# Second layer of a hybrid backbone: four gate projections of the first merge emitted inside the attention

## The chip, the cores and the metric

The kernel runs on one core of a Trainium2 chip. The metric is the device time of one execution in microseconds; lower is better. Engines are named as in the profile: PE is TensorE's matmul, PEld its weight load, DVE is VectorE, ACT is ScalarE, POOL is GpSimd, SP is the engine that issues the large loads.

## The reference

Two layers over 256 latent tokens and 256 context tokens, with a model width of 1024. Each layer has a mixing sub-layer with three branches on one normalised and modulated input h, and a convolutional feed-forward network. In the second (last) layer only the latent tokens go on, so most products have 256 columns there. The part that the change touches:

```python
cq, ckv, kr, uf, ur, ug, gl = split_in(h @ w_in)       # gl: 3 x 1024 gate logits
att = blocked_attention(q, k, v)                       # 8 heads, from cq, ckv, kr
g_att, g_f, g_rnn = split(sigmoid(gl), 3)
y = (g_att * (att @ w_o_attn)
     + g_f * (fourier_mix(uf) @ w_o_fourier)
     + g_rnn * (((h_f + h_b) * gelu(ug)) @ w_o_rnn)) @ w_out
```

fourier_mix is the real part of a two-dimensional DFT over positions and group channels; h_f and h_b come from gated linear recurrences over the tokens in both directions. All is float32; the kernel gets the precision on PE by splitting each operand into a rounded high part and a low part and adding three products.

## The kernel before

**Products.** gemm (L138) issues three matmuls per 128 rows of the contraction: high x high, high x low and low x high. A weight tile goes through three steps: load (L174) brings it from memory into one of three raw buffers by a load on SP's queue, and those loads are kept in program order (L165); unit (L193) takes one of three weight buffers (wp, wh and wl in the profile) and wsplit casts it on ACT (wh, L152) and subtracts on DVE (wl, L159); project (L605) multiplies eight such row blocks with h, 24 matmuls, into a bank of PSUM. columns (L199) loads 256 columns of a weight matrix at once, 1 MB, and gives two units of 128 columns, the second only when it is asked for.

**Order.** The program is written as generators, and what stands earlier in the program has the higher priority. A planner orders each engine's instructions at build time from its own estimates of time and from when buffers come free; on the chip each engine then keeps its fixed order. So an instruction that is emitted earlier is a candidate earlier; it isn't bound to the place where it stands.

**Second layer, attention (L861).** Eight heads, in four pairs p, are pipelined: step k of the loop emits the scores of head k (sc, then the softmax: nmx, pr, rs), the transposes of head k-1 (pt, split into pth and ptl) and the weighted values of head k-2 (pv, split into ath and atl). The one PSUM bank for pv is taken in turns. In steps 1, 3 and 5 the next pair's keys (kn) and queries (proj with nh, nl) are emitted with raised priority, with loads for their weights; step 3 also emits the second half of the values (v). At the end of step k, emit(fill, FILLS[l].get(k, 0)) (L974) advances a filler generator by so many steps. The filler is features (L762): the projection uf for the Fourier branch, in two halves of 256 columns; a half is three steps, one for the load and its two weight units, and one for each of two blocks of 128 tokens with 24 matmuls. For the second layer the table FILLS (L44) puts the first half into step 2 and the second half into step 8:

```python
FILLS = ({12: 1}, {2: 3, 8: 3})
```

**Second layer, branches (L1155).** fourier (L784) loads the DFT matrices (dft_l, dft_c), splits them (dlh, dll, dch) and forms fa and ff. Then recurrent (L979) runs beside the first two merges: each of its steps emits a gated recurrence (products gt, then tanh, exp, square root and scans on ACT, DVE and POOL) and the next convolved input (L996: two products with 512 and 256 columns, whose loads are issued at L1002); after it two steps of the merges follow. A step of merge (L1078) has two gate projections with tanh (sg, L1086), the product of the branch with two of its output tiles, and their product with the gate. The first merge is the Fourier branch's; its gates go straight into the eight M tiles. The attention's merge follows, and last the recurrence's. run(first_two, recurrent(rnn), 2) sets these two steps of merge per recurrence, so the first merge's first two steps (mp 0 and 1) go with the first recurrence.

**Memory.** phase (L94) opens tagged tiles in SBUF; the branches reuse the space of the attention's tiles. banks (L105) does the same for PSUM: three banks mm, two sc, one pt and one pv in the attention; three mg and four rc in the branches.

Of the kernel before, what the change touches and what calls it, by code (L numbers as in the profile page):

```python
# [12 lines left out]
F32 = mybir.dt.float32  # L13
F32R = mybir.dt.float32r
AF = mybir.ActivationFunctionType
# [4 lines left out]
D = 1024  # L20
# [18 lines left out]
C_UF, C_UR, C_UG, C_GL = 672, 1184, 1696, 2208  # L39
# [1 line left out]

HELD = (5, 8)

FILLS = ({12: 1}, {2: 3, 8: 3})  # L44


def constants():
# [23 lines left out]
def backbone(ctx: ExitStack, tc: tile.TileContext, a: dict, out: bass.AP):  # L71
    nc = tc.nc
# [7 lines left out]
    def nm(s):  # L80
        count[0] += 1
        return f"{s}_{count[0]}"
# [3 lines left out]
    def slot(s, tag="n", dtype=F32R, w=512):  # L86
        pool, bufs, tag = where[tag]
        return pool.tile([P, w], dtype, tag=tag, name=nm(s), bufs=bufs)

    def pair(s, tag, w=512):  # L90
        return slot(s + "h", tag, w=w), slot(s + "l", tag, w=w)

    @contextmanager
    def phase(name, **tags):  # L94

        with tc.tile_pool(name=nm(name), bufs=1, reuse_waits="tile") as pool:
            was = {t: where.get(t) for t in tags}
            where.update({t: (pool, n, t) for t, n in tags.items()})
            yield
            where.update(was)  # L100
# [14 lines left out]
    def bank(s, tag=None):  # L115
        pool, t, n = bank_of[tag or s]
        return pool.tile([P, 512], F32, tag=t, name=nm(s), bufs=n)
# [50 lines left out]
    def chain(*gens):  # L168
        for g in gens:
            yield from g  # L170
# [3 lines left out]
    def load(src, kt, c):  # L174
        if ticks:
            ticks[0]()
        return chunk(src.rearrange("(k p) c -> p k c", p=P), kt, c)
# [15 lines left out]
    def unit(v, tag=None):  # L193
        h, lo = wunit(v.shape[1], v.shape[2], tag)
        wsplit(h, lo, v)
        wmode["n"] += 1
        return h, lo

    def columns(w, c0, c1):  # L199

        kt = w.shape[0] // P
        for c in range(c0, c1, 256):
            n = min(256, c1 - c)
            v = load(w[:, c : c + n], kt, n)
            for j in range(0, n, P):
                yield unit(v[:, :, j : j + P])

    def run(main, side=None, every=1):

        while True:  # L210
            left = side is not None and next(side, True) is None
            for _ in range(every):
                if next(main, True) is not None and not left:
                    return
# [390 lines left out]
    def project(u, xs, r, parts=None, tag="mm"):  # L605

        hv, lv = u
        o = bank("proj", tag)[:, 0 : r.stop - r.start]
        for q in parts or [r]:
            oq = o[:, q.start - r.start : q.stop - r.start]  # L610
            gemm(oq, [(hv[:, k, :], lv[:, k, :], xs[k][0][:, q], xs[k][1][:, q]) for k in range(len(xs))])
        return o
# [4 lines left out]
    def mixer(l, col, ada_cols, last, h, tiles_of, steps, squares, first, then, open_banks):  # L617
        t0 = CTX if last else 0
        W = T - t0
        NS = W // CTX  # L620
        X, Y = slice(t0, T), slice(0, W)
        w_in = a["w_in"][l]
# [139 lines left out]
        def features(U, tag, where):  # L762

            for half in range(2):
                v = load(w_in[:, C_UF + half * 256 : C_UF + (half + 1) * 256], 8, 256)
                us = [unit(v[:, 0:4, :]), unit(v[:, 4:8, :])]
                yield
                f = slice(half * 256, (half + 1) * 256)
                for i in range(W // P):
                    r = slice(t0 + i * P, t0 + (i + 1) * P)  # L770
                    o = bank("uf", where)[:, 0:256]
                    gemm(
                        o,
                        [
                            (h[k][0][:, r], h[k][1][:, r], us[k // 4][0][:, k % 4, :], us[k // 4][1][:, k % 4, :])
                            for k in range(8)
                        ],
                    )
                    if half == 0:
                        U.append(pair("U", tag))  # L780
                    split(U[i][0][:, f], U[i][1][:, f], o)
                    yield
# [67 lines left out]
        def query_weights(p):  # L850
# [7 lines left out]
                wsplit(u[0][:, :, d0 : d0 + w], u[1][:, :, d0 : d0 + w], v[:, :, c0 : c0 + w])  # L858
            return u

        def attention(att, cq, ckvn, keys, pre, fill):  # L861
            vals, heads, cqn = {}, {}, []

# [96 lines left out]
            for k in range(len(items) + 2):  # L960
# [11 lines left out]
                if k == per + 1:  # L972
                    values(1, *kv)
                emit(fill, FILLS[l].get(k, 0))  # L974
                if k >= 2:
# [97 lines left out]
                    tile_0 = tile_1  # L1073
                    yield

        M, merged = [None] * 8, []

        def merge(b, br, wo, gofs):  # L1078

            for mp in range(4):  # L1080
                gu = columns(w_in, gofs + mp * 256, gofs + (mp + 1) * 256)
                sg = []
                for _ in range(2):
                    o = project(next(gu), h, X, None, "mg")
                    g = slot("sg", "M" if b == 0 else "sg", F32, W)
                    nc.scalar.activation(g, o, AF.Tanh, scale=0.5)  # L1086
                    sg.append(g)
                wu = unit(load(a[wo][l][:, mp * 256 : (mp + 1) * 256], 4, 256))
                for z in range(2):
                    m = 2 * mp + z  # L1090
                    c = slice(z * P, (z + 1) * P)
                    o = project((wu[0][:, :, c], wu[1][:, :, c]), br, Y, None, "mg")
                    g = sg[z]
                    nc.vector.scalar_tensor_tensor(g, g, 1.0, o, op0=ALU.add, op1=ALU.mult)
                    if b == 0:
                        M[m] = g
                    elif b == 1:
                        nc.gpsimd.tensor_tensor(M[m], M[m], g, op=ALU.add)
                    else:
                        nc.vector.tensor_tensor(M[m], M[m], g, op=ALU.add)  # L1100
                        hi, lo = slot("mh", "br", w=W), slot("ml", "att", w=W)
                        split(hi, lo, M[m])
                        merged.append((hi, lo))
                yield
# [21 lines left out]
        att, rnn, lats = [], [], []  # L1126
# [6 lines left out]
            next(lat)  # L1133
            yield
        U = []
        with phase("mix", att=8, **(dict(U=4) if last else {})):
            if last:
                tags = dict(rope=2, key=8, val=4, cqn=6, ckvn=4, q=6, pr=4, pt=8)
            else:
                tags = dict(rope=2, key=8, val=6, cqn=6, ckvn=4, q=4, pr=4, pt=4)  # L1140
            with phase("mla", **tags):
                load_rope()
                next(lat)
                lat_banks.close()
                with banks(dict(rb="mm", ss="mm"), mm=3, sc=2, pt=1, pv=1):
                    fill = features(U, *(("U", "mm") if last else ("M", "mg")))
                    run(attention(att, *lats, fill))
                    if last:
                        emit(fill)
            tags = dict(M=8, br=16 if last else 12)  # L1150
            if last:
                inner = dict(rg=1, sg=2, gw=4, u=6, ri=7, av=3, hd=4, ug=1)
            else:
                inner = dict(rg=1, sg=2, gw=2, u=3, ri=4, av=2, hd=2, ug=1)
            with phase("branch", **tags), banks(dict(rb="mg", ss="mg", out="rc"), mg=3, rc=4):  # L1155
                with phase("inner", **inner):
                    if not last:
                        emit(fill)
                    four = fourier(U)
                    if not last:  # L1160
                        wmode["hi"] = [nc.vector]
                    if last:
                        spread(steps, 0.5)
                    first_two = chain(merge(0, four, "w_o_fourier", C_GL + D), merge(1, att, "w_o_attn", C_GL))
                    run(first_two, recurrent(rnn), 2)
                    wmode["hi"] = [nc.scalar]
                    run(merge(2, rnn, "w_o_rnn", C_GL + 2 * D))
                    emit(steps)
                    ticks.clear()
                    units = ahead(out_units(), 2)  # L1170
                with phase("out", wo=2 * (8 - HELD[l])):
                    project_out(units)
# [233 lines left out]
    h = [pair("h", "h") for _ in range(8)]  # L1406
# [3 lines left out]
    def first_tiles(part):  # L1410
# [8 lines left out]
    mix = mixer(  # L1419
        0, columns_of[0], adas[0], False, h, first_tiles, chain(par0, ada(0, 1), ada(0, 2)), sq_ffn,  # L1420
        lambda: ups.append(ahead(columns(a["w_up"][0], 0, DFF))), lambda r: then[0](r), lambda: lat_banks,
    )
# [34 lines left out]
    for b in range(1, 3):  # L1457
# [9 lines left out]
    mix = mixer(  # L1467
        1, columns_of[1], adas[1], True, h_mix, lambda half: None, iter(()), sq_ffn,
        lambda: ups1.append(ahead(columns(a["w_up"][1], 0, DFF))), to_ffn, latent_banks,
    )  # L1470
# [29 lines left out]
```

## Time and profile before

| what | value |
|---|---|
| runs without profile | 1379.17, 1380.52, 1381.95 us; median 1380.52 us |
| the profiled execution, its own time | 1378.18 us |
| span of its profile | 1376.4 us |
| busy share of the span: PE, PEld, DVE, ACT, POOL | 97%, 83%, 68%, 50%, 15% |

The span runs from the first to the last instruction of the profiled execution; all positions below are microseconds from its start. In it the second layer's attention lies at about 918 to 991 us, the Fourier branch's DFT at 991 to 998, the recurrence and the first two merges at 998 to 1109, the third merge and the output projection behind that until 1172. A matmul's end is modelled, so its duration in a row (0.28 us for 256 columns) is longer than the distance from one start to the next.

### The profile page before, as it was taken

Reading aid. Unit: us, or ns where it says so; the run is one execution under the profiler, and the core shown is the slowest. Engines: PE = TensorE matmul, PEld = TensorE weight load, DVE = VectorE, ACT = ScalarE, POOL = GpSimd, SP = SyncE. Lnnn points to the kernel's source line nnn. Section 1 sums busy time; section 2 is a strip of 40 time slices with the busy share of each in tenths; the row PEclk is TensorE's granted clock in tenths of the full one; section 3 lists DMA queues with packets and bytes.
Section 4 is the critical chain, followed back from the end, with each engine's and each line's share of the span. In section 5 each row is a group of like instructions: output and inputs, shape, how many; then the busy total and the mean of one; then the engine's idle time right before and its main releaser. Section 6 shows DMA issues by size and latency. Waiting matters only on the chain.

```text
span 1376.4 us, 20199 instructions
## 1 busy us (share of the span) xinstructions
PE 1338.5 (97%) x7949; PEld 1148.8 (83%) x7949; DVE 931.7 (68%) x1528; ACT 688.9 (50%) x1165; POOL 200.8 (15%) x194
## 2 busy tenths in 40 slices
PE   7999999999999999999999999999999999999997
PEld 6777698888888798888888787978899999999996
DVE  3587646567644555579976786659777776766666
ACT  5476625335522434444421235457587855655555
POOL 2020002002120040101100011201012322111111
PEclk9999999999999999999999999999999999999999
DMA  9433652323233412245567764221255556455551
GB/s 330 141 104 143 247 152 65 112 80 92 81 104 107 153 36 93 92 135 171 152 183 252 269 214 131 72 73 52 71 156 146 165 156 210 150 189 179 189 189 72
DMA packets 177472, 196.42 MB, mean 143 GB/s; under 512 B 9285, under 2 KB 155699, under 8 KB 175329
## 3 DMA queue, kind: packets, MB, share of 16 engines
q1 hardware_dynamic: 176048, 193.23, 43.9%
q0 software_dynamic: 1328, 1.90, 0.4%
q8 instruction: 62, 1.02, 0.3%
q14 instruction: 34, 0.27, 0.1%
HBM read 194.06 MB, written 1.05 MB: 142 GB/s over the span
## 4 chain that ended last, share of the span: by engine, by line
PE 79%; DVE 9%; DMA 6%; ACT 4%; issue 2%; POOL 0%; SPq 0%; ACTq 0%; DVEq 0%; POOLq 0%
PE proj L130 49%; PE out L130 7%; PE acc L130 4%; DMA raw<-in_w_ada_dram 4%; PE lat L130 4%; DVE wl L159 3%; PE uf L130 2%; PE pa L130 2%; PE pv L130 2%; PE gt L130 1%; PE sc L130 1%; DVE acc L453 1%; PE pt L924 1%; DVE hf L564 1%; ACT wh L152 1%
## 5 line engine op out<-in xcount | busy, mean ns | idle before, releaser
L159 DVE TENSOR_TENSOR wl<-raw,wh 128x1024 fp32r<-128x1024 f32 (+9 forms) x337 | 336.9, 1014 | 154.6 <-ACT wh L152 152.0
L130 PE MATMUL proj<-hh,wl 128*128 128x512 f32 (+1 forms) x1232 | 415.1, 337 | 2.1 <-DVE wl L159 2.1
L130 PE MATMUL proj<-hh,wh 128*128 128x512 f32 (+1 forms) x1232 | 415.4, 338 | 0.0
L130 PE MATMUL proj<-hl,wh 128*128 128x512 f32 (+1 forms) x1232 | 414.9, 337 | 0.0
L152 ACT CAST wh<-raw 128x1024 fp32r<-128x1024 f32 (+7 forms) x305 | 248.1, 837 | 258.4 <-PE proj L130 149.9
L130 PEld LDWEIGHTS proj<-hh,wl 128*128 128x128 f32 x1232 | 233.6, 190 | 27.8 <-DVE wl L159 3.2
L130 PEld LDWEIGHTS proj<-hh,wh 128*128 128x128 f32 x1232 | 233.5, 190 | 25.5 <-issue 0.8
L130 PEld LDWEIGHTS proj<-hl,wh 128*128 128x128 f32 x1232 | 233.6, 190 | 25.4 <-DVE hl L566 0.2
L1370 POOL TENSOR_TENSOR gate<-gate,up 128x512 f32<-128x512 f32 (+1 forms) x44 | 57.7, 1312 | 460.2 <-ACT gate L1369 446.0
L453 DVE SCALAR_TENSOR_TENSOR acc<-raw,cvec,acc 128x512 f32<-128x512 f32 x112 | 88.6, 808 | 9.8 <-DMA raw<-in_w_ada_dram 8.6
L159 DVE TENSOR_TENSOR gTl<-gate,gTh 128x512 fp32r<-128x512 f32 (+1 forms) x44 | 24.4, 555 | 51.1 <-ACT gTh L152 51.0
L1369 ACT ACTIVATE gate<-gate 128x512 f32<-128x512 f32 (+1 forms) x44 | 23.1, 524 | 71.5 <-DVE gate L1225 71.5
L531 POOL TENSOR_TENSOR sq<-sq,sq 128x256 f32<-128x256 f32 (+1 forms) x22 | 26.2, 1189 | 176.5 <-ACT sq L529 176.4
L152 ACT CAST gTh<-gate 128x512 fp32r<-128x512 f32 (+1 forms) x44 | 22.6, 514 | 49.6 <-POOL gate L1370 49.6
L130 PE MATMUL out<-mh,wl 128*128 128x256 f32 (+1 forms) x152 | 47.4, 312 | 0.0
L130 PE MATMUL out<-ml,wh 128*128 128x256 f32 (+1 forms) x152 | 47.4, 312 | 0.0
L130 PE MATMUL out<-mh,wh 128*128 128x256 f32 (+1 forms) x152 | 47.4, 313 | 0.0
L154 DVE CAST wh<-raw 128x1024 fp32r<-128x1024 f32 x32 | 22.3, 698 | 33.3 <-PE proj L130 32.7
L130 PE MATMUL down<-gTh,wh 128*128 128x512 f32 x112 | 44.0, 393 | 0.0
L130 PE MATMUL down<-gTh,wl 128*128 128x512 f32 x112 | 43.7, 390 | 0.0
L130 PE MATMUL down<-gTl,wh 128*128 128x512 f32 x112 | 43.6, 389 | 0.0
L130 PE MATMUL lat<-hh,wh 128*128 128x512 f32 (+3 forms) x108 | 39.0, 361 | 0.6 <-ACT hh L565 0.6
(312 smaller groups left out, 2720.9 us busy)
## 6 DMA issues: line engine op xcount, KB each, us to landing
raw<-in_w_up_dram SPq DMA_DIRECT2D x44, 1024.0 KB, 5.1
raw<-in_w_ada_dram SPq DMA_DIRECT2D x40, 1024.0 KB, 5.3
raw<-in_w_in_dram SPq DMA_DIRECT2D x30, 1024.0 KB, 5.5
raw<-in_w_down_dram SPq DMA_DIRECT2D x11, 1024.0 KB, 4.9
raw<-in_w_ada_dram SPq DMA_DIRECT2D x32, 256.0 KB, 7.2
raw<-in_w_in_dram SPq DMA_DIRECT2D x16, 512.0 KB, 4.7
raw<-in_w_out_dram SPq DMA_DIRECT2D x8, 1024.0 KB, 5.3
raw<-in_w_down_dram SPq DMA_DIRECT2D x8, 896.0 KB, 5.3
```

Of the source, the lines that this page charges most:

```text
L130: pinned(nc.tensor.matmul(o, lhsT, rhs, start=start, stop=stop))
L152: nc.scalar.copy(out, in_)
L154: eng.tensor_copy(out, in_)
L159: (lo_eng or nc.vector).tensor_tensor(lo, src, hi, op=ALU.subtract)
L453: nc.vector.scalar_tensor_tensor(accs[z], w, sc, accs[z], op0=ALU.mult, op1=ALU.add)
L531: eng.tensor_tensor(self.terms[0][:, r], self.terms[0][:, r], sq[:, r], op=ALU.add)
L564: nc.vector.scalar_tensor_tensor(f[:, r], xr[j][:, r], g, rb, op0=ALU.mult, op1=ALU.mult)
L924: nc.tensor.transpose(o[:, c], probs[i][:, kt * P : (kt + 1) * P], ident)
L1369: nc.scalar.activation(g, g, AF.Gelu_apprx_tanh)
L1370: nc.gpsimd.tensor_tensor(g, g, us[z], op=ALU.mult)
```

## The change

A generator early_gates computes the first merge's gates for the columns C_GL + D to C_GL + D + 512, which are the four projections of its steps mp 0 and mp 1, with their tanh, into four tiles of a new tag eg. mixed takes steps from features (f) and from early_gates (g) by a plan. The table then gives: step 2 of the attention the first Fourier half (fff), step 5 one gate, step 6 the second Fourier half, step 8 one gate, step 9 two gates. merge takes these gates from a list where it has them, and loads and projects the rest; the tag M has four tiles where it had eight. The first layer is as it was.

```diff
-FILLS = ({12: 1}, {2: 3, 8: 3})
+PLAN = "fffgfffggg"
+FILLS = ({12: 1}, {2: 3, 5: 1, 6: 3, 8: 1, 9: 2})
...
+        def mixed(a, b, plan):
+            for x in plan:
+                next(a if x == "f" else b, None)
+                yield
...
-        M, merged = [None] * 8, []
+        M, merged, early = [None] * 8, [], []
+
+        def early_gates(n, tag):
+
+            gu = columns(w_in, C_GL + D, C_GL + D + n * 256)
+            for _ in range(2 * n):
+                o = project(next(gu), h, X, None, "mm")
+                g = slot("sg", tag, F32, W)
+                nc.scalar.activation(g, o, AF.Tanh, scale=0.5)
+                early.append(g)
+                yield
...
             for mp in range(4):
                 gu = columns(w_in, gofs + mp * 256, gofs + (mp + 1) * 256)
-                sg = []
-                for _ in range(2):
+                sg = [early.pop(0) for _ in range(2)] if b == 0 and early else []
+                while len(sg) < 2:
                     o = project(next(gu), h, X, None, "mg")
...
-        with phase("mix", att=8, **(dict(U=4) if last else {})):
+        with phase("mix", att=8, **(dict(U=4, eg=4) if last else {})):
...
                     fill = features(U, *(("U", "mm") if last else ("M", "mg")))
+                    if last:
+                        gates = early_gates(2, "eg")
+                        fill = mixed(fill, gates, PLAN)
                     run(attention(att, *lats, fill))
                     if last:
                         emit(fill)
-            tags = dict(M=8, br=16 if last else 12)
+            tags = dict(M=4 if last else 8, br=16 if last else 12)
```

## Rows read from the trace of the kernel before

**Rows 1.** Busy time by stretch: start:end, length, each engine (instructions), granted clock, DMA share, GB/s.

```profile
957.00:973.00 16.00, 14.46 (x102) 12.53 (x100) 15.35 (x34) 9.71 (x24) 1.45 (x2) 1.00 0.03 10
973.00:998.00 25.00, 22.77 (x170) 20.23 (x168) 15.68 (x33) 12.97 (x30) 1.89 (x3) 1.00 0.38 97
998.00:1014.70 16.70, 16.70 (x98) 14.80 (x98) 12.57 (x16) 10.71 (x16) 4.31 (x4) 1.00 0.54 162
1014.70:1043.40 28.70, 28.70 (x207) 27.15 (x206) 20.97 (x29) 23.28 (x32) 4.88 (x4) 1.00 0.53 152
...
1071.90:1108.70 36.80, 35.10 (x268) 33.66 (x267) 28.55 (x36) 35.56 (x47) 14.20 (x12) 1.00 0.42 129
1108.70:1172.00 63.30, 63.30 (x525) 63.11 (x525) 42.42 (x59) 31.67 (x50) 13.43 (x10) 1.00 0.63 200
```

**Rows 2.** Waits of PE, 957 to 998 us: total us, times, longest.

```profile
PE pv L130 <- DVE atl L159: 2.0, 2, 1.0
PE fa L130 <- ACT dlh L152: 0.9, 1, 0.9
PE pt L924 <- DVE ptl L159: 0.5, 1, 0.5
```

**Rows 3.** Waits of PE, 998 to 1172 us, and of ACT, 1014.7 to 1043.4 us.

```profile
PE proj L130 <- DVE wl L159: 1.7, 1, 1.7
...
ACT wh L152 <- PE proj L130: 6.4, 3, 3.9
```

**Rows 4.** Groups of PE instructions, 957 to 998 us: one of three alike, and the transposes.

```profile
L924 PE MATMUL pt<-ident,pr 128*128 128x128 f32 x40 | 6.4, 282 | 0.5 <-DVE ptl L159 0.5
...
L130 PE MATMUL sc<-kh,qh 128*128 128x512 f32 x8 | 3.5, 434 | 0.2 <-ACT qh L152 0.2
...
L130 PE MATMUL kn<-nh,wh 128*128 128x512 f32 x2 | 0.8, 396 | 0.0
```

**Rows 5.** Timeline of PE: start, duration, instruction; distances from start to start.

```profile
981.67 0.65 PE L924 MATMUL pt<-ident,pr 128*128 128x128 f32 x4
982.09 0.36 PE L130 MATMUL uf<-wh,hh 128*128 128x256 f32 x1
...
999.20 0.39 PE L130 MATMUL proj<-hh,wl 128*128 128x512 f32 x1
999.43 0.39 PE L130 MATMUL proj<-hh,wh 128*128 128x512 f32 x1
```

**Rows 6.** Timeline, ACT, DVE and PE, 955 to 971 us; idle before, and what ended it.

```profile
955.12 1.05 ACT L152 CAST wh<-raw 128x1024 fp32r<-128x1024 f32 x1 [1.14 <-DMA raw<-in_w_in_dram]
...
957.29 2.78 DVE L159 TENSOR_TENSOR wl<-raw,wh 128x96 fp32r<-128x96 f32 x5
...
960.58 0.33 PE L130 MATMUL pv<-pth,vh 128*64 128x256 f32 x1 [1.05 <-DVE atl L159]
...
970.59 1.23 DVE L159 TENSOR_TENSOR wl<-raw,wh 128x1024 fp32r<-128x1024 f32 x1
```

**Rows 7.** Groups of ACT instructions, 1014.7 to 1043.4 us: busy us, mean ns | idle before.

```profile
L152 ACT CAST wh<-raw 128x1024 fp32r<-128x1024 f32 x9 | 9.4, 1043 | 6.5 <-PE proj L130 6.4
```

**Rows 8.** Timeline of SP's queue: the second Fourier half's load, and the recurrence's first four.

```profile
949.49 0.37 SPq L165 DMA_DIRECT2D raw<-in_w_in_dram  x1
...
978.46 14.99 SPq L1002 DMA_DIRECT2D raw<-in_w_in_dram  x4
```

**Rows 9.** Timeline of ACT: an Exp, and a gate's tanh right behind it.

```profile
1020.19 0.81 ACT L1037 ACTIVATE av<-ri,cneg 128x512 f32<-128x512 f32 x1
1020.91 0.36 ACT L1086 ACTIVATE sg<-proj 128x256 f32<-128x256 f32 x1
```

**Rows 10.** Loads issued by SP: count, KB each, us from issue to landing.

```profile
raw<-in_w_in_dram SPq DMA_DIRECT2D x16, 512.0 KB, 4.7
```

**Rows 11.** Matmuls of the Fourier projection, both layers: durations, first and last start.

```profile
L130 PE MATMUL uf<-wh,hl x96: 278/283/362, 175.5 to 986.6; 128*128 128x256 f32 x96
```

## Prediction

> **What bounds the kernel now.** I read the table of busy time by stretch first, for the second layer from the second half of its attention to the end of its merges [rows 1]. From 1014.7 to 1172 us TensorE is the bound: with 256 columns it issues 525 matmuls in 63.3 us, one every 0.1206 us, its weight loads fill 63.11 of those 63.3 us, and the stretch from 1014.7 to 1043.4 has no idle PE at all. The lists of waits [rows 2, 3] say the same: between 998 and 1172 PE waits once, 1.7 us for a weight split on DVE. In the attention it is different. From 957 to 973 DVE works 15.35 of 16 us, and from 957 to 998 PE is idle for 1.5 + 2.2 = 3.8 us. The granted clock is 1.00, that is 2.4 GHz, in all of these stretches, so no term of the sum is a clock.
>
> How much room has PE from 957 to 998? Three measures. The idle time gives 3.8 us; it is too low, since a matmul's modelled end (0.28 us) hides part of each stop. Counting gives more: of 272 matmuls [rows 1], three kinds of scores with 8 each and three kinds of key products with 2 each are 512 wide [rows 4], 30 in all at 0.23 us (999.20 to 999.43 in [rows 5]); 40 are transposes, at 0.42 us for four (981.67 to 982.09); the other 202 take 0.1206. That is 6.9 + 4.2 + 24.4 = 35.5 us of issue in 41 us: **5.5 us of gaps**. The third measure is 41 less the weight loads, 41 - 12.53 - 20.23 = 8.2 us; it is too high, because a 512-wide matmul outlasts its weight load. I take 5.5, and keep 3.8 and 8.2 for the range. The Trainium skill (Perfetto Trace Analysis, Identifying the Most-Contended Engine) says that matmul busy time is no good measure of how near PE is to its limit and that the share of weight loads is; by it the room would be 8.2, and the merges, at 63.11 of 63.3, would be full, which the rows show too.
>
> **The change part by part.**
> 1. Four projections leave the first two steps of the first merge and go into the attention: 4 x 24 matmuls x 0.1206 = 11.6 us of PE. They leave a stretch in which PE never waits (1014.7 to 1043.4 holds both steps), so all 11.6 us are saved there. In the attention they cost 11.6 less the gaps that they fill. Moving alone is worth nothing.
> 2. Gaps filled. The waits behind the 5.5 us are known: pv for DVE's atl twice (2.0 us), fa for ACT's dlh once (0.9), pt for ptl (0.5) [rows 2], the rest is the refill after each. What lies ready at those points is new: one gate from about 960, the Fourier half from about 970 (two heads earlier than now), three gates until the end. I let one stop stay, the first, at 960.58 (1.05 us idle [rows 6]): there DVE works through five splits in 2.78 us ahead of atl, and the first gate's own split comes out of that row, so its matmuls aren't ready before. **5.5 - 1.1 = 4.4 us filled.**
> 3. The weight splits: per gate a cast of 1.04 us on ACT [rows 7] and a subtraction of 1.23 us on DVE (970.59 in [rows 6]), 4.9 us more for DVE, which is nearly full until 973. A rotation of three weight buffers decides when they come. The Fourier half's first unit is cast at 955.12 as soon as its load lands; its second is subtracted at 970.59, when the last key and value products have given a buffer back. After the change the first gate stands ahead of it on the queue and takes the place at 955; the Fourier units follow at about 969 to 971; the other gates come after them, when DVE is idle (25 - 15.68 = 9.3 us from 973 to 998). So only one more split falls before 973, where DVE has 0.65 us left: 0.6 us over. PE has the first gate and the Fourier half (48 matmuls, 5.8 us) for cover, so I cost it at 0; without that cover it costs 0.6, and with two splits 1.8.
> 4. Loads. Two loads of 1 MB move on SP's queue to ahead of the Fourier half and ahead of the DFT matrices; everything behind them (dft_l, dft_c, the recurrence's small weights, its first columns) moves back a place. At 949.49 a load has to wait for one of three raw buffers [rows 8], and ACT then waits 1.14 us for its landing [rows 6]. The gate's load now has that place and the same size: 0. The Fourier half comes right behind; it is needed some 19 us later: 0. The recurrence's first load is the rival below.
> 5. The tanh of a gate (0.36 us [rows 9]) is queued among the attention's casts on ACT and holds those behind it: 1.4 us in all, on an engine with 41 - 9.71 - 12.97 = 18.3 us free: 0. An Exp is followed by a tanh at 1020.91 without a table load between [rows 9], so none is added. The tiles (four more here, four fewer in the merge) cost nothing that runs.
> 6. The stretch that gets lighter. Two merge steps and a recurrence had 28.7 us of PE and 23.28 us of ACT [rows 1]; they keep 17.1 of PE, and ACT keeps 23.28 - 4 x 1.04 - 4 x 0.36 = 17.7. The cover of the recurrence is gone: ACT is now as long as PE. The cost lies between 0 (ACT has 16.7 - 10.71 = 6.0 us free just before, to cast ahead) and 17.7 + 6.4 - 17.1 = 7.0, if the 6.4 us in which ACT now waits for PE to return weight buffers [rows 3] stayed whole. The nearest row is the stretch from 1071.9 to 1108.7, where ACT is at 35.56 of 36.8 us and PE loses 1.7. In 17 us that is 0.8; I take **1.0 us lost**.
>
> Sum: -4.4 + 1.0 = **-3.4 us**. The profiled execution took 1378.18 us (span 1376.4), which gives 1374.8; the median of the runs shown is 1380.52, 2.34 above, so I forecast **1377.1**.
>
> **Rivals.**
> - *More: every gap is filled* and ACT casts ahead, so that term 6 is 0: -5.5, at most -8.2; 1374 or so. For it: PE has three kinds of filler where it had one. Against: the order is fixed at build time, and a filler can stand behind the waiting instruction. Chance 0.12.
> - *No change: DVE sets the pace up to 973*, or the planner leaves the gates at the attention's end, where they do what they did before. With two splits before 973 that stretch grows by 2 x 1.23 - 0.65 = 1.8, its own gaps stay, and only the 2.2 us of 973 to 998 are filled: -2.2 + 1.8 + 1.0 = +0.6, 1381.1. For it: DVE's 15.35 of 16. Against: behind 973 DVE is idle for 9.3 of 25 us, and three of the four gates come there. The Trainium skill (Perfetto Trace Analysis, Identifying the Most-Contended Engine) would speak against the change: it names the engine with the highest occupancy as the one to relieve first, and here that engine is given more; by that rule the time is this rival's. Chance 0.26.
> - *Slower: the recurrence's first columns come late.* Their load was issued at 978.46 [rows 8], into a raw buffer that was free; now that buffer holds the second gate load, until the last gate's split. With t the end of that split, the columns are ready at t + 4.7 (landing of 512 KB [rows 10]) + 1.04 + 1.23 = t + 7.0. PE's own work lasts to 957 + 35.5 + 11.6 = 1004.1. Up to t = 997 the wait costs nothing, beyond it all of it, and from t = 1003 the kernel is measurably slower. With t = 1004, were the last gates cast only behind the DFT, 7 us are lost: +3.6, 1384.1. For it: the four issues at 978.46 take 14.99 us already, since the second pair waits for a raw buffer. Against: the last gates need only the Fourier half's buffers, which come free with the last uf matmul at 986.6 [rows 11], so t is about 991. Chance 0.18.
>
> **How the numbers follow.** The forecast has 0.44 (its own range -1.5 to -5.5, 1375 to 1379). The range takes in the larger gain and most of the slower case: 1372.5 to 1383; outside are a fill by the third measure and a long wait. A measurement of this kernel can tell about 0.2%, 2.8 us, from no change. Most of the forecast (0.37) and the larger gain (0.12) lie beyond that: faster 0.5. The rest of the forecast, the second rival and a little of the third: same 0.31. Most of the third: slower 0.19.
>
> **What would show it.** Right: the second half's uf matmuls ahead of the scores of the last two heads; gate matmuls between the pv groups where PE waited for atl and dlh; the stretch from the first recurrence product to the third convolution shorter by 10 to 11 us with PE full; the first convolution's matmuls without a DMA wait. Wrong: the waits for atl and dlh still there with the same length; a wait of PE for wl or for the load of the recurrence's columns at the start of the branch; ACT full and PE waiting for wl in the first recurrence. If the merges shrink by 11 us and the attention grows by 11, term 2 is wrong; if the attention grows by 7 and the merges shrink by 7, term 6 is.

## The result, and the profile after

The changed kernel takes 1387.24 us (median of 8 runs, 1384.91 to 1388.65) against 1380.95 us before (8 runs beside it): a ratio of 1.0053 with a 95% interval of 1.0042 to 1.0064. It is slower by about 7 us, where 3.4 us of gain were forecast; the time lies above the range.

In what follows a run is told in three stages, by starts of matmuls: from the first scores of the second layer (931.54 us before, 931.55 after) to the first convolution of the recurrence, from there to the first gt product, and from there to the first matmul of the output projection. The first convolution counts from where its matmuls run on without matmuls of the DFT between. Ahead of the first scores the profiled executions differ (930.4 to 934.3 us) although their program is the same there, so stages are compared, not spans. Before, the three are 66.43 + 16.75 + 134.04 = 217.22 us; after, 77.68 + 18.51 + 128.84 = 225.03. So the attention and the DFT grow by 11.25 us (11.6 us of matmuls came in), the start of the recurrence by 1.76, and the merges, which lost those 11.6 us, give back only 5.20.

The table of busy time by stretch after, with the columns of [rows 1]: the first gt is at 1027.74, the next ones at 1044.73, 1079.58 and 1099.86.

```profile
957.00:973.00 16.00, 14.37 (x98) 12.08 (x97) 15.32 (x32) 10.29 (x25) 1.45 (x2) 1.00 0.24 69
973.00:1000.30 27.30, 27.30 (x219) 26.32 (x218) 16.60 (x30) 13.85 (x30) 2.23 (x2) 1.00 0.06 16
1000.30:1009.20 8.90, 6.59 (x51) 5.87 (x49) 2.90 (x6) 3.63 (x8) 0.52 (x1) 0.99 0.57 143
1009.20:1027.70 18.50, 18.44 (x96) 15.68 (x97) 13.36 (x17) 11.57 (x18) 3.98 (x4) 0.91 0.77 209
1027.70:1044.70 17.00, 17.00 (x110) 15.45 (x109) 15.27 (x22) 15.98 (x20) 2.30 (x3) 1.00 0.43 131
1044.70:1079.60 34.90, 30.86 (x207) 28.43 (x206) 23.51 (x30) 23.95 (x34) 5.75 (x6) 0.95 0.41 121
1116.50:1179.90 63.40, 63.39 (x525) 63.10 (x525) 42.42 (x59) 31.67 (x50) 13.52 (x11) 1.00 0.64 200
```

Until 973 nothing was filled: 14.37 us of PE in 16 us, 14.46 before [rows 1]. From 973 on PE is full, so the late gates and the Fourier half cover each other. The first recurrence's period shrank from 28.5 to 17.0 us, as PE's work did; but the second period, in which nothing was changed, grew from 28.5 to 34.9 us at the same 207 matmuls. The last line is the control: as before.

The waits of PE after, 957 to 1172 us (in all, times, longest), to be read against [rows 2, 3]:

```profile
PE proj L131 <- DVE wl L160: 4.1, 2, 2.4
PE proj L131 <- ACT wh L153: 1.7, 2, 1.4
PE pv L131 <- DVE atl L160: 1.1, 1, 1.1
PE fa L131 <- ACT dlh L153: 0.9, 1, 0.9
PE gt L131 <- DVE u L1019: 0.8, 1, 0.8
PE pt L930 <- DVE ptl L160: 0.5, 1, 0.5
PE gt L131 <- ACT gug L1023: 0.4, 1, 0.4
```

Of the waits of the attention one atl is gone; dlh, ptl and the other atl stayed. From the first convolution on there were 1.7 us of waits and there are now 7.0 us (4.1 + 1.7 + 0.8 + 0.4); 1.4 of these stand at the convolution itself, 5.6 in the merges.

**The start of the recurrence.** POOL's and SP's timeline after, then ACT's and PE's, at the place where the recurrence's first columns are loaded:

```profile
1000.54 0.52 POOL L989 MEMSET rg<- 128x512 f32 x1 [23.99 <-PE pv L131]
...
1001.09 1.26 SPq L996 DMA_DIRECT2D rg<-in_rg_w_a_dram  x2
1002.40 1.26 SPq L996 DMA_DIRECT2D rg<-in_rg_w_x_dram  x2
1003.76 2.25 SPq L1008 DMA_DIRECT2D raw<-in_w_in_dram  x3
...
1008.12 1.04 ACT L153 CAST wh<-raw 128x1024 fp32r<-128x1024 f32 x1 [2.65 <-DMA raw<-in_w_in_dram]
...
1009.22 0.80 PE L131 MATMUL proj<-hh,wh 128*128 128x512 f32 x1 [1.36 <-ACT wh L153]
1009.81 0.63 PE L131 MATMUL proj<-hl,wh 128*128 128x512 f32 x1
```

The chain stands there from top to bottom. A memset of the tile rg waits 24 us for the last pv product; the loads into rg wait for the memset, and the columns' loads, behind them on SP's queue, come at 1003.76 where they were issued at 978.46 [rows 8]. PE waits 1.36 us for their cast. Then two 512-wide matmuls stand 0.59 us apart in place of 0.23 [rows 5]: from 1009 to 1013 the mean granted clock is 0.57, so for most of these 4 us it is at its lower level, 1.2 GHz.

**The second period.** ACT, DVE and PE after, 1059 to 1068 us:

```profile
1059.06 1.28 ACT L1052 ACT_TABLE_LOAD   x1
1060.36 1.15 ACT L1052 ACTIVATE ri<-ri 128x512 f32<-128x512 f32 x2
1061.53 1.28 ACT L1102 ACT_TABLE_LOAD   x1
1062.82 0.39 ACT L1102 ACTIVATE sg<-proj 128x256 f32<-128x256 f32 x1
1063.11 1.04 ACT L153 CAST wh<-raw 128x1024 fp32r<-128x1024 f32 x1
...
1064.07 0.75 DVE L1058 TENSOR_TENSOR_SCAN ri<-av,ri,ri 128x256 f32<-128x256 f32 x1
1065.74 0.42 DVE L1064 TENSOR_TENSOR y<-y,gug 128x256 f32<-128x256 f32 x1 [0.93 <-POOL y L1063]
1066.09 1.22 DVE L160 TENSOR_TENSOR wl<-raw,wh 128x1024 fp32r<-128x1024 f32 x1
...
1067.36 0.58 PE L131 MATMUL proj<-fh,wl 128*128 128x256 f32 x1 [2.42 <-DVE wl L160]
1067.74 0.41 PE L131 MATMUL proj<-fh,wh 128*128 128x256 f32 x1
```

PE needs a weight whose high part ACT casts only at 1063.11, behind two table loads; its low part then stands on DVE behind the recurrence's scans and y. PE waits 2.42 us, and the matmuls after it come every 0.21 us in place of 0.12 (mean granted clock 0.76 from 1064 to 1070).

### The profile page after: what moved, and what is told of

The parts are those of the page before. It is cut to its first block, busy times and chain, and to the rows that moved or that the text cites. A ratio compares the mean times of both kernels' runs of the same rounds, so it can differ in the third digit from the quotient of the medians.

```text
span 1385.2 us, 20188 instructions
## 1 busy us (share of the span) xinstructions
PE 1342.0 (97%) x7949; PEld 1151.2 (83%) x7949; DVE 933.7 (67%) x1528; ACT 688.1 (50%) x1164; POOL 199.9 (14%) x194
## 5 line engine op out<-in xcount | busy, mean ns | idle before, releaser
L160 DVE TENSOR_TENSOR wl<-raw,wh 128x1024 fp32r<-128x1024 f32 (+9 forms) x337 | 337.0, 1013 | 150.5 <-ACT wh L153 148.0
L131 PEld LDWEIGHTS proj<-hh,wl 128*128 128x128 f32 x1232 | 234.5, 190 | 28.5 <-DVE wl L160 3.8
L566 ACT ACTIVATE hh<-hf,ada 128x256 fp32r<-128x256 f32 x56 | 26.1, 503 | 25.6 <-DVE hf L565 25.1
```

Source lines behind the costliest of these rows:

```text
L131: pinned(nc.tensor.matmul(o, lhsT, rhs, start=start, stop=stop))
L160: (lo_eng or nc.vector).tensor_tensor(lo, src, hi, op=ALU.subtract)
L566: nc.scalar.activation(h[0][:, r], f[:, r], AF.Identity, bias=b)
```

## The experiments

"e3" and so on are the runs' names. All have the kernel before beside them on the same chip (medians 1378.6 to 1380.8). Stages in us:

| run | to the first convolution | to gt | to the output projection | sum | ratio to before, interval |
|---|---|---|---|---|---|
| before | 66.43 | 16.75 | 134.04 | 217.22 | |
| after | 77.68 | 18.51 | 128.84 | 225.03 | 1.0053 [1.0042, 1.0064] |
| e1 half at step 6 | 70.29 | 16.74 | 134.06 | 221.09 | 1.0023 [1.0012, 1.0034] |
| e2 layout alone | 68.05 | 19.99 | 134.01 | 222.05 | 1.0039 [1.0026, 1.0052] |
| e3 columns first | 76.54 | 15.63 | 128.90 | 221.07 | 1.0036 [1.0023, 1.005] |
| e4 steps 3,2,2,1 | 77.46 | 18.61 | 128.89 | 224.96 | 1.0059 [1.0044, 1.0074] |
| e7 gates of 0 and 2 | 76.74 | 15.63 | 131.18 | 223.55 | 1.005 [1.0033, 1.0067] |
| e8 e7, half at 8 | 77.11 | 15.63 | 131.74 | 224.48 | 1.0066 [1.005, 1.0083] |
| e9 two gates | 71.55 | 15.63 | 133.49 | 220.67 | 1.0028 [1.0015, 1.0041] |
| e10 two gates late | 71.97 | 15.63 | 133.25 | 220.85 | 1.0019 [1.0006, 1.0032] |
| e11 gelu in four tiles | 76.95 | 15.63 | 131.26 | 223.84 | 1.0044 [1.0032, 1.0057] |
| e12 first gate on POOL | 79.38 | 15.63 | 130.19 | 225.20 | 1.0064 [1.0049, 1.008] |
| e13 e11, casts on POOL | 76.91 | 15.63 | 128.81 | 221.35 | 1.0022 [1.001, 1.0034] |
| e14 before, gelu in four tiles | 66.46 | 16.74 | 138.19 | 221.39 | 1.0034 [1.0022, 1.0047] |
| e15 e3, casts on POOL | 76.55 | 15.63 | 130.55 | 222.73 | 1.0051 [1.0036, 1.0067] |
| e16 gates in bank e | 78.62 | 15.63 | 129.97 | 224.22 | 1.0045 [1.0026, 1.0063] |
| e17 e15 and e16 | 78.57 | 15.63 | 129.24 | 223.44 | 1.0064 [1.0045, 1.0082] |
| e18 before, casts on POOL | 66.58 | 17.95 | 137.93 | 222.46 | 1.0055 [1.0039, 1.007] |
| e19 POOL casts, two periods | 76.74 | 15.63 | 127.69 | 220.06 | 1.0012 [1.0001, 1.0023] |
| e20 every second cast | 76.73 | 15.61 | 128.17 | 220.51 | 1.0011 [0.9998, 1.0024] |

In e3 and the runs built on it (e7 to e13, e15 to e17, e19, e20) the columns are there so early that five of the first convolution's 24 wide matmuls run among those of the DFT; this is the first of them in e3:

```profile
1004.11 0.40 PE L131 MATMUL proj<-hh,wh 128*128 128x512 f32 x1
1004.35 0.28 PE L131 MATMUL ff<-ah,dch 128*128 128x256 f32 x1
```

They count in the first column there, and 15.63 is 16.75 without them. So for what the attention hides, the first two columns belong together.

**Why the columns come late: e2 and e3.** e2 is the kernel before with the tiles of the change and nothing moved; e3 is the changed kernel with the first columns' loads ahead of rg.

```diff
# e2, against before
-        with phase("mix", att=8, **(dict(U=4) if last else {})):
+        with phase("mix", att=8, **(dict(U=4, eg=4) if last else {})):
...
-            tags = dict(M=8, br=16 if last else 12)
+            tags = dict(M=4 if last else 8, br=16 if last else 12)
...
-                    g = slot("sg", "M" if b == 0 else "sg", F32, W)
+                    g = slot("sg", ("eg" if last and mp < 2 else "M") if b == 0 else "sg", F32, W)
# e3, against after
+            first_u = convolved(0) if last else None
             rg = slot("rg", "rg", F32)
             nc.gpsimd.memset(rg, 0.0)
...
-            tile_0 = (*gate_weights(0), *convolved(0))
+            tile_0 = (*gate_weights(0), *(first_u or convolved(0)))
```

> The kernel before with the change's memory layout alone: the four tiles eg lie ahead of the attention's tiles and M has four, but the gates are computed in the merge as before. Theory A (the attention's tiles lie 4 KB further on, so the tile rg now shares its place with a value tile, its memset waits for the last pv, and SP's queue holds the recurrence's columns behind it): memset right after the last pv near 990.6 us, first columns issued some 3 us later, first convolution matmul near 999.5 us in place of 998.0, and 1.5 to 4 us over before with the low clock that follows. Theory B (the columns are late since the second gate load holds a raw buffer): no change, within 1 us of before.

> The changed kernel with the first convolution emitted ahead of the recurrence's small weights in the second layer, so that SP issues its columns without waiting for the memset of rg. Theory A: columns issued near 988 us when the last gate's split gives a raw buffer back, no wait at the first convolution and no low clock behind it, 3 to 4 us less than the changed kernel, so 2 to 3.5 us over before. Theory B: the columns stay as late as they were and the time stays at 6 us over before.

The memset before; the memset and PE's first convolution in e2; the memset in e3:

```profile
975.23 0.53 POOL L983 MEMSET rg<- 128x512 f32 x1
```

```profile
989.83 0.52 POOL L983 MEMSET rg<- 128x512 f32 x1 [15.44 <-PE pv L130]
...
998.46 0.79 PE L130 MATMUL proj<-hh,wh 128*128 128x512 f32 x1 [1.26 <-ACT wh L152]
```

```profile
985.39 0.53 POOL L1016 MEMSET rg<- 128x512 f32 x1 [9.41 <-PE sc L131]
```

The tiles alone cost 4.8 us. By their sizes, four tiles eg move the attention's tiles by 4 KB while the recurrence's pool doesn't move, so that rg comes to lie on a tile that the last pv still reads; the addresses are in no trace, but pv is what the memset waits for, where before it ran at 975.23 without a wait. The wait is the smaller part: the start of the recurrence lasts 3.2 us longer, with a mean granted clock of 0.51 from 998 to 1005. With the columns ahead of rg (e3), PE goes from the DFT into the convolution without a stop and 4.0 us come back. The edit changes the place of rg too (its memset now waits for a product of scores), but the columns' loads, issued at 987.49, no longer stand behind it. The raw buffer, the cause that the third rival gave, isn't needed to explain the loss: e2 moves no gate and has it.

**What the attention fills: e1, e8, e10, e12, e16.**

```diff
# e1, against before
-FILLS = ({12: 1}, {2: 3, 8: 3})
+FILLS = ({12: 1}, {2: 3, 6: 3})
# e8, against e7 (below)
-FILLS = ({12: 1}, {2: 3, 5: 1, 6: 3, 8: 1, 9: 2})
+FILLS = ({12: 1}, {2: 3, 5: 1, 8: 4, 9: 2})
# e10, against e9 (below)
-PLAN = "fffgfffg"
-FILLS = ({12: 1}, {2: 3, 5: 1, 8: 3, 9: 1})
+PLAN = "ffffffgg"
+FILLS = ({12: 1}, {2: 3, 8: 3, 9: 2})
# e12, against e11 (below)
-            for _ in range(2 * n):
-                o = project(next(gu), h, X, None, "mm")
+            for i in range(2 * n):
+                wmode["lo"] = [nc.gpsimd if i == 0 else nc.vector]
+                u = next(gu)
+                wmode["lo"] = [nc.vector]
+                o = project(u, h, X, None, "mm")
# e16, against e3
-                o = project(next(gu), h, X, None, "mm")
+                o = project(next(gu), h, X, None, "e")
```

> The kernel before with the second Fourier half in step 6 in place of step 8, and no gate in the attention. The theory (the loss comes from the late recurrence columns and from the lightened first recurrence) expects no loss here: within 1 us of before, the memset of rg near 975 us, no wait for the first columns. The rival that the earlier Fourier half lengthens the attention expects 2 us or more over before, with the last pv later than at 990.6 us.

> e7 with the second Fourier half back at the end of step 8, the gates as they were (one at 5, one behind the half at 8, two at 9). Theory (by e1, taking the half to step 6 leaves the attention's tail without filler, 2.7 us at the last pv): the first convolution 1.5 to 3 us earlier than in e7 and e3 (1007.96), at 1005 to 1006.5; median 1.5 to 3 us below e7's. Rival (the three late gates are filler enough, and the half at 6 serves): first convolution within 0.7 us of e7's.

> e9 with both gates at step 9, behind the whole Fourier projection. If the gate at step 5 has no use there because its weight split waits for a weight buffer until 973 (as it did in the changed kernel), the first convolution is within 0.7 us of e9's. If the early gate fills gaps of heads 4 to 6, it is 1 to 2 us later here; if it delays the Fourier half and the softmax's casts, 0.5 to 1.5 us earlier.

> e11 with the low part of the first early gate's weights subtracted on POOL in place of DVE. If it was DVE's full queue that kept the first gate from the gaps of 957 to 970 (in the changed kernel its high part is cast at 955.5, its low part subtracted at 970.9), the gate's first matmuls come at 959 to 965, and the first convolution 1 to 2 us earlier than in e11. If it was a weight buffer that comes free late, no matmul of the gate before 970 and the first convolution within 0.5 us of e11's. The merges as in e11.

> e3 with the early gates in PSUM bank e, which is idle in the attention, in place of the three banks mm. e12 had the first gate's weights ready at 960.6 and still no matmul of it before 974. If it is the bank mm that comes late (values, keys and queries hold the three until DVE has split them), the first gate's matmuls come at 960 to 966, the idle times of PE from 957 to 970 (2.5 us) fall below 1.2, and the first convolution is 0.8 to 2 us earlier than in e3 (76.54 us from the first scores). If it is neither, as in e3 within 0.4 us; one bank for four gates could also hold the later ones: up to 1 us later.

e1 missed what I expected: the half alone at step 6 costs 3.9 us. It fills nothing earlier and the tail loses its filler; PE's waits for ptl go from [rows 2]'s 0.5 us, once, to 2.9 us in four:

```profile
PE pt L924 <- DVE ptl L159: 2.9, 4, 1.2
```

With gates in the tail, the half's place is worth nothing (e8 and e7 0.4 apart), and neither is the place of the first gate (e10 and e9 0.4 apart). So of 11.6 us that came in, how much is hidden? From the first scores to gt e3 takes 92.17 us, before 83.18: it grows by 9.0, so 2.6 are hidden, though gaps of 5.5 were counted. Summed from start to start of the matmuls, the gaps up to 973 are 2.3 us before and 2.4 in e3; from there to the last pv 3.3 before and 1.1 in e3; the stop for dlh is 1.0 in both; in the DFT it is 0.5 and 0.1, filled by the convolution's five matmuls and not by a gate. So the gates and the half filled most of the gaps between 973 and the last pv, and none before. Why not? The gate's weights were ready in time: in the changed kernel DVE subtracts them in the row of five splits that ends at 960.42 (one of the five is 128x1024). The text for e12 took the row at 970.9 for it, wrongly; that is the next unit. Yet its first matmul is at 973.15. e12 shows the same with POOL, and e16 shows what it waits for:

```profile
958.22 2.40 POOL L160 TENSOR_TENSOR wl<-raw,wh 128x1024 fp32r<-128x1024 f32 x1 [14.65 <-ACT wh L153]
...
976.23 0.28 PE L131 MATMUL proj<-hh,wh 128*128 128x256 f32 x1
```

```profile
965.71 0.28 PE L131 MATMUL proj<-hh,wh 128*128 128x256 f32 x1
...
972.37 0.39 PE L131 MATMUL v<-wh,nh 128*128 128x256 f32 x1 [0.86 <-DVE vl L160]
```

In e12 weights that are ready at 960.6 wait until 976.23 (and the attention takes 2.4 us longer than in e11, 79.38 for 76.95, with PE waiting 1.2 us for POOL's ql and 1.5 for vl); in e16, with a PSUM bank of its own, the gate starts at 965.71, counted from the first scores 8.5 us earlier than in the changed kernel. The banks mm were the reason for the late start. But the attention gets 2.1 us longer, not shorter: the last values come 3.8 us later, counted in the same way, and all that hangs on the next pair, its keys, queries and scores, comes later with them. As I read this order, not as a run tests it: the stops of 957 to 970 are places where a chain through DVE is late, and 2.9 us of gate matmuls put into a stop of 0.5 us (for ptl) push the chain on.

**What the merges give back: e4, e7, e9, e11, e14.** Is it the order of the light steps (e4), the length of a recurrence (e7, e9), or the single gelu tile (e11, with e14 as control)? (e9 has two tiles eg and six M, and the Fourier half back in step 8.)

```diff
# e4, against after
-                    run(first_two, recurrent(rnn), 2)
+                    for _, n in zip(recurrent(rnn), (3, 2, 2, 1) if last else (2, 2, 2, 2)):
+                        emit(first_two, n)
# e7, against e3
-            gu = columns(w_in, C_GL + D, C_GL + D + n * 256)
+            cs = [C_GL + D + mp * 256 for mp in (0, 2)]
+            gu = chain(*[columns(w_in, c, c + 256) for c in cs])
...
-                sg = [early.pop(0) for _ in range(2)] if b == 0 and early else []
+                sg = [early.pop(0) for _ in range(2)] if b == 0 and early and mp % 2 == 0 else []
# e9, against e3
+PLAN = "fffgfffg"
+FILLS = ({12: 1}, {2: 3, 5: 1, 8: 3, 9: 1})
...
-                        gates = early_gates(2, "eg")
+                        gates = early_gates(1, "eg")
...
# e11, against e3; e14, against before
-                ug = slot("gug", "ug", F32, W)
+                ug = slot("gug", "U", F32)[:, 0:W] if last else slot("gug", "ug", F32, W)
```

> The changed kernel with three merge steps behind the first recurrence, then two, two and one, in place of two each, so that the two light steps and one full one lie beside it. Theory C (with the four gates gone the first recurrence has 17 us of PE work beside a chain of 20 us on ACT and DVE, so PE waits in the second period and loses clock): the waits near 1046 and 1064 us go, 4 to 6 us less than the changed kernel, 0 to 2.5 us over before. Rival (ACT's total work sets these waits, whatever the order): no change against the changed kernel, or more wait in the last recurrence.

> e3 with the four early gates taken from the first merge's steps mp 0 and mp 2 in place of 0 and 1, so that the first two recurrences each lose 5.8 us of TensorE work in place of 11.6 in one. From the first recurrence product to the start of the output projection: 134.0 us before, 128.9 in e3 and e4. Theory D (a recurrence's own chain of ACT, DVE and POOL takes some 22 to 25 us, whatever stands beside it, so a period can't shrink by 11.6 but can by 5.8): 122.5 to 125 us here, periods of 22.7 to 24.5, median 1378.5 to 1381. Rival E (whatever is taken out of the merges, some 6 us come back, since the total of loads and casts up to the output projection sets the end): 128.9 again, median 1384.5.

> e3 with two early gates (mp 0 alone: one at step 5, one at step 9; two tiles eg, six M) and the half at step 8. Theory D: only the first period is lighter, by 5.8, and keeps all of it: from the first recurrence product to the output projection 128.2 to 129.3, as much as with four gates of mp 0 and 1. The first convolution at 997.98 + 5.8 - 1 to 3 us of filled gaps, 1000.8 to 1002.8. Median 1377.5 to 1380.5. Rival E (each gate is worth half in the merges): 131 us, median 1381 to 1383.

> e3 with the recurrence's gelu tile (gug, one buffer) put into the four tiles U, which nobody reads any more by then. Theory F (a recurrence takes 18.3 us from its first gt product to y, as the changed kernel shows at 1027.7 to 1046.05; a period of 17.0 is shorter, so the next gelu, with one tile, waits for y on ACT and holds the casts of the next recurrence behind it): the idle time at the start of the second period (2.2 us in e3 from 1042 to 1045) goes, and from the first gt to the output projection it takes 125 to 127.5 us, 128.9 in e3; median 1381.5 to 1383.5. Rival G (ACT's queue of casts and table loads in the second period holds PE, whatever the gelu does): 128.4 or more, the 2.6 us before a weight's low part in the second period still there.

> The kernel before with the gelu tile in the tiles U, as in e11: a control. There gelu follows y without a wait and PE is full, so both theories expect no change: 134.0 us from the first gt to the output projection, median within 0.2% of the kernel before. If it is faster by more, e11's gain says nothing of the early gates.

All of these theories fell in the form they had. The order of the steps changes nothing (e4). Spread over two periods, as many gates give back less (e7: 131.18), and two gates next to nothing (e9: 133.49, 0.55 of 5.8 us). The timeline of e9's ACT, and PE behind it:

```profile
1028.09 1.28 ACT L1053 ACT_TABLE_LOAD   x1
1029.38 0.63 ACT L1053 ACTIVATE ri<-ri 128x512 f32<-128x512 f32 x1
1030.03 1.28 ACT L1103 ACT_TABLE_LOAD   x1
1031.33 0.38 ACT L1103 ACTIVATE sg<-proj 128x256 f32<-128x256 f32 x1
1031.73 1.28 ACT L1053 ACT_TABLE_LOAD   x1
1033.02 0.63 ACT L1053 ACTIVATE ri<-ri 128x512 f32<-128x512 f32 x1
1033.56 2.92 ACT L153 CAST wh<-raw 128x1024 fp32r<-128x1024 f32 x3
...
1034.64 0.50 PE L131 MATMUL proj<-hh,wh 128*128 128x512 f32 x1 [2.13 <-ACT wh L153]
```

In this plan a gate's tanh stands between the two square roots: five table loads in the period where before there were four, and PE waits 2.13 us for the cast behind them. e7 has the same order in both of its lighter periods, ten loads where before there were eight. e11 and e14 say something alike in another way: more tiles for gelu cost 2.4 us beside the gates and 4.2 us without them (PE's gt then waits 2.7 us for gug in e14), so the planner uses the freedom for an order that is worse. They don't test the single tile, which stays open.

**ACT's queue: e13, e15, e18, e19, e20, and all together: e17.** Every third weight cast beside the recurrences goes to POOL; in e19 beside the first two alone, in e20 there every second.

```diff
+                    if last:
+                        wmode["hi"] = [nc.scalar, nc.scalar, nc.gpsimd]
                     run(first_two, recurrent(rnn), 2)
```

> e11 with every third weight cast beside the recurrences on POOL in place of ACT. Rival G (ACT's queue holds PE): from the first gt to the output projection at least 1.5 us less than in e11, if POOL's cast takes no more than some 3 us. Theory F alone: as e11, within 0.7 us. If POOL takes longer than that, PE waits for POOL's casts and it is more than e11.

> e3 with every third weight cast beside the recurrences on POOL (1.22 us each in e13) and the gelu tile as it was. Rival G (ACT's queue holds PE in the lighter stretch): from the first gt to the output projection 1.5 to 4 us below e3's 128.9, as e13 stood 2.45 below e11; median 1380.5 to 1383. If what e13 saved was only made good of e11's own loss (131.26 to 128.81), this stays at 128.9 and ACT's queue isn't the cause.

> The kernel before with the same casts on POOL: a control. PE is full there from 998 to 1072, so nothing is gained in the merges' first two periods (134.0 from the first gt to the output projection, less the 1.7 us that PE waits at 1108 at the most); median within 0.2% of the kernel before.

> e16 and e15 together, the version that the two theories make the best: the sum of the two savings, 2.5 to 5 us below e3; median 1378.5 to 1382, so at or a little below the kernel before.

> e15 with the casts on POOL only beside the first two recurrences; from the third on all are on ACT again. In e15 the first two periods took 49.1 us (e3 51.9) but the stretch behind the fourth recurrence 61.1 (e3 56.7). If ACT's queue is what holds PE in the light stretch: the first two periods 48.5 to 49.8 and the rest as in e3 (20.3 and 56.7), 125.5 to 127 in all; median 1381 to 1383. If the 2.8 us come back behind the second recurrence whatever is done, 128.5 or more.

> e19 with every second cast on POOL in place of every third. If ACT's queue still holds PE there: the first two periods below e19's by 0.7 to 2 us. If what is left of the loss is the recurrence's own chain (gelu waiting for y, gt waiting for u), as in e19 within 0.5; if POOL's casts (1.25 us each, beside its share of the recurrence) are late in their turn, more.

In the first two periods the casts on POOL bring 2.9 us in e13 (50.0, e11 52.9) and 2.8 in e15 (49.1, e3 51.9); in the control, where PE is full, they cost 0.8 (57.8, before 57.1). That is what ACT's queue as the cause asks for. But each edit lets the planner order all engines anew, and that alone can be worth as much: e15 and e19 put the same casts on POOL in these two periods and yet differ by 1.6 us (49.1, 50.7). The gain has one sign in four runs (e13, e15, e19, e20) and the other in the control; its size isn't shown more closely, and that a new order is part of it isn't ruled out. The 2.42 us for wl of the changed kernel are 0.60 in e19. But in e15 and e18 the stretch behind the fourth gt grows from 56.7 to 61.1 and 59.8 us (in e18 PE waits 2.3 us for a gate's tanh), so the totals missed. Where POOL is kept out of that (e19), 127.69 remains, 1.2 below e3: above the 127 that I had set as bound, as its first two periods, at 50.7 us, are above 49.8. What PE waits for then is the recurrence itself, at the start of e19's second period (in e15 the same two stops):

```profile
1042.26 0.50 PE L131 MATMUL gt<-uuh,gwh 128*128 128x512 f32 x1 [0.82 <-ACT gug L1009]
...
1045.20 0.71 PE L131 MATMUL gt<-uuh,gwh 128*128 128x512 f32 x1 [1.39 <-DVE u L1005]
```

More casts on POOL (e20) take a further 1.0 us out of these periods (49.7, e19 50.7), and lose 1.5 behind the fourth gt. e17 adds the bank, and its loss. e19 is the best version with early gates, level with e20; neither beats the kernel before.

## Why the prediction was wrong

The sum was -3.4 us; the stages say +7.8. The 11.2 us between are three steps, of 4.0, 1.8 and 5.4 us:

- **Term 5, "The tiles (four more here, four fewer in the merge) cost nothing that runs"**, was wrong by 4.0 us (after 225.03, e3 221.07). I had counted the tiles' bytes, not their addresses: what lies on whose place decides when a later tile may be written, and SP's queue handed that wait on to the columns. The third rival had the right place and sign (columns late, DMA wait at the start of the branch) with the wrong cause; its t, the last gate's split, plays no part.
- **Term 2, 4.4 us of gaps filled**, measured 2.6 (e3), 0.4 of them by the first convolution and not by a gate. (The gaps were 6.2 us rather than 5.5: among the 272 matmuls those that overlap the ends of a stretch count twice.) The step that failed is that what is ready can fill: up to 973 no gap shrank. Half of what I called ready was so: the weights were, from 960. I had not asked which PSUM bank the product would take, and the banks mm were taken until 973. Nor would the bank alone have helped (e16, 2.1 us longer): I had counted as free room what reads there as the lateness of a chain. The measure by weight loads, 8.2, that the Trainium skill (Perfetto Trace Analysis, Identifying the Most-Contended Engine) suggests, was further off still.
- **Term 6, 1.0 us lost in the lighter stretch**, measured 6.4 (11.6 - 5.2), inside its bounds of 0 and 7.0, near the upper one; the row of 1071.9 that I called nearest was not. In e3, where the matmuls' distances were summed over the two periods, the 6.5 us are four stops of 4.7 us together and 1.8 us in longer distances, most of them behind the last stop (granted clock 0.68 from 1064 to 1068). Supported: with every third cast off ACT's queue 1.2 to 2.9 us of it go (e13, e15, e19 and the control), with the planner's new order as a possible part of that. Seen in waits, not shown by an experiment: gt waiting for gelu and u at the recurrence's turn. The loss is not where I looked for it: the first period is as short as PE's work (17.0), and the next one pays.
- The sentence that no term of the sum is a clock failed with these steps: the clock was 1.00 before, but by the changed kernel's rows (0.57 over 4 us, 0.76 over 6 us) the lower level costs about 1.7 and 1.4 us behind two of the waits, an estimate that is contained in the terms above.

Terms 3 and 4 as such held: one more split before 973 and the Fourier half's load cost nothing that e3 shows, though the cover that term 3 counted on, a gate and the half, came only behind 973. That moving the half is free was implied and was wrong alone (e1, 3.9 us), right with gates behind it (e8). The second rival, with the rule of the Trainium skill (Perfetto Trace Analysis, Identifying the Most-Contended Engine) to optimize the busiest engine first, forecast no change. The kernel is slower, and not by DVE's work, which is 15.32 of 16 us up to 973 where it was 15.35. In the merges the busiest was PE, and with 11.6 us less for it ACT stands at 15.98 of 17.0 us.

## What to carry to other kernels

Work moved off a full engine is worth what the next engine leaves: read the second busiest queue's order (table loads, in-order splits, scans) for the stretch as it will be, and look one stage further than the one that got lighter. Before a gap is counted as room, ask what is late there, which buffer and bank the filler needs, and whether the filler is longer than the gap. A new tile moves the addresses of others; find which tile its successors now lie on, and what is queued behind the first write.

## What the runs showed of the hardware

A short stop of PE can cost more than itself, in clock: behind 1.36 us of waiting the mean granted clock was 0.57 over the next 4 us (after), behind 1.26 us 0.51 over 7 us (e2). The length of the stop does not decide it: 1.7 us of waiting at 1108.7 in the kernel before were followed by 1.00 [rows 1, 3], and so was the stop of 0.9 us for dlh in e3 (1.00 from 1000.9 to 1007.9). Ahead of its fall in the changed kernel PE had been busy for 6.59 of 8.9 us (1000.3 to 1009.2); what decides stays open. POOL casts 128x1024 in 1.22 us (e13), about ACT's 1.04 [rows 7], but subtracts the same size in 2.40 (e12) where DVE takes 1.22.
